# Leftover modulation weights loaded as 1 MB pairs during the routing, and the norm steps on Pool taken one block at a time

## The chip, the cores and the metric

The kernel runs on one core of a Trainium2 chip. The metric is device time in microseconds (us): the median of three runs of the kernel before is 2188.16 us, from 2187.27 to 2190.72. Durations below come from one profiled execution of its own.

## The reference, cut to what matters

Two transformer blocks run one after the other on 256 tokens of width 1024, all in fp32.

The first block is a mixer (mLSTM and Hyena) followed by an expert-choice mixture of experts: 16 experts, each of which takes its 32 best tokens. Its shifts, scales and gates are "modulations", a conditioning vector times a 1024 x 6144 matrix.

The second block has depth 2 and two streams, a latent stream `x` (the output of the first block) and a context stream of 256 tokens that does not depend on `x`. For every layer and both streams there are six modulation groups of 1024 values:

```python
mod = (silu_c @ w_ada[l] + b_ada[l])[:, None, :]
mod_c = silu_cc @ w_ada[l] + b_ada[l]
...
x = layer_norm(ALPHA * x + g1 * (o @ w_out[l]), ln1_g[l], ln1_b[l])
x = layer_norm(ALPHA * x + g2 * swiglu(modulate(x, sh2, sc2), w_ffn_in[l], w_ffn_out[l]), ln2_g[l], ln2_b[l])
```

## The kernel before, in words

The work has three stages.

**Phase A** (`phase_a`, up to 262 us of the span) is the mixer of the first block. TensorE multiplies from 1 MB weight tiles, tag `w`, a ring of 4 buffers. `gemm2` inserts background steps with `bg(2)`: each step is one `next` of the generator `later`, that is, one 128 x 1024 slice of a modulation matrix. A step loads 512 KB with `mtile` (L805, issued at L396 in `wtile`) into the ring `wm` of 4 buffers (in phase A also `wx`, 2 buffers) and multiplies it in 4 matmuls (L406). Eight steps make a group, which ends in `modout` and `modend`: an ACT copy `mrow`, two transposes, two small DVE additions. A group and its end share the single PSUM buffer "f". `later` has 12 groups, 96 steps; phase A takes 74 of them. The last 22 (six of one group, and two whole groups) are left for `ctx_path`, which runs them first (`yield from self.later`).

**The experts.** `moe_route` (L1045) computes the router's softmax, picks the 32 best tokens of each expert in a chain of small DVE operations with four PE transposes, and gathers the tokens into `xsel` with 32 matmuls. Then `moe` walks the 16 experts: 24 weight tiles of 1 MB each, 384 in all, loaded by `etile` (L1107) into 7 buffers in turn (4 of tag `w`, 3 of tag `wb`, the latter in memory that phase A gives back at its end). `run` interleaves the context stream: `ctx_path` is a generator whose steps carry costs, and after each of the first 366 expert tiles it is advanced to a share of `total`, 524.4 units; the 22 leftover steps count 0.5 each. A context step is put behind the expert tile's last matmul with `issue_after`.

**The latent stream** (`x_path`) runs after the last expert. In its feed-forward (`ffn`, L1808), 22 hidden blocks of 128 columns are computed one after the other. TensorE works in 48 fp32r matmuls on a block, after ACT (`wh`) and DVE (`wl`) have split its weights in a high and a low half. The end of a block is `fin(j, pp)`: DVE forms `lt` from PSUM, ACT writes the silu to `hj` (2 buffers), DVE multiplies into `hj`, ACT copies its high half to `hidh`, and Pool subtracts it to get the low half, `hidl`, in `evac` (L256). Only then is the `hj` buffer free. With each `fin`, `next(app)` traces one step of `apply` (L1338): three Pool operations that normalise one of 8 blocks of the residual `xT`, for use much later in the second half of the feed-forward. Nothing but the tracing order stands between these operations and the `hidl` ones.

All weight loads are issued from the one in-order queue of SP. Instructions of an engine run in the order in which the scheduler put them; `issue_after(ins)` puts what it encloses behind `ins` on the same engine, with no wait of its own.

Of the kernel before, what the change touches and what calls it, by code (L numbers as in the profile page):

```python
# [218 lines left out]
class _B:  # L219
# [104 lines left out]
    def T(self, pool, shape, tag, bufs=1, dt=F32):  # L324
        self.n += 1
        return pool.tile(shape, dt, tag=tag, name=f"{tag}_{self.n}", bufs=bufs)
# [72 lines left out]
    def modvec(self, psp, wd, lhs, bias, outs, groups, get=None):  # L399

        for g in groups:
            ps = self.P(psp)
            for k in range(8):
                w = get(g, k) if get else self.mtile(wd[128 * k:128 * k + 128, 1024 * g:1024 * g + 1024])
                for c in range(4):
                    self.mm(ps[32 * c:32 * c + 32, 0:256], lhs[:, k, :], w[:, 256 * c:256 * c + 256], k == 0, k == 7)  # L406
                yield 0.5
            self.all(self.modout(self.wm, psp, ps, bias, outs, g))
# [36 lines left out]

    def run(self):
        nc, tc, d = self.nc, self.tc, self.d
        self.wbufs = {"w": 4, "wm": 4, "wx": 2, "wb": 3, "wd": 2, "split": 4}
        with ExitStack() as es:
            E = lambda **k: es.enter_context(tc.tile_pool(**k))  # L450
            self.cp = E(name="cp", bufs=1)
            self.res = E(name="res", bufs=1)
            pm, pa = "b", "a"
            self.ws = E(name="ws", bufs=5, side="right")
            with tc.tile_pool(name="ps", bufs=1, space=PSUM) as self.pp, \
                    tc.tile_pool(name="wm", bufs=4, side="right") as self.wm:
                self.pbufs = {"b": 2, "a": 3, "g": 2, "f": 1}
                self.setup()
                with tc.tile_pool(name="A", bufs=1) as ap:
                    self.wx = ap  # L460
                    self.phase_a(ap, pm, pa)
                    self.wx = None
                if self.stop == "A":
                    return
                kp = E(name="kv", bufs=1)
                self.kvpool(kp)
                with tc.tile_pool(name="M", bufs=1) as mp, tc.tile_pool(name="WB", bufs=1) as self.wb:
                    self.moe_route(mp, pm)
                    with tc.tile_pool(name="X", bufs=1, side="right") as xp:

                        g = self.ctx_path(xp, pa)
                        done, total = 0.0, 524.4
                        for i, _ in enumerate(self.moe(mp, pm)):
                            while done < total * (i + 1) / 366:

                                with tc.issue_after(self.elm.ins):
                                    c = next(g, None)
                                if c is None:
                                    break
                                done += c  # L480
                        for c in g:
                            done += c
            if self.stop == "X":
                return
            self.pbufs = {"g": 2, "l": 2, "s": 2, "t": 1, "o": 1}
            with tc.tile_pool(name="ps2", bufs=1, space=PSUM, reuse_waits="tile") as self.pp, \
                    tc.tile_pool(name="C", bufs=1, reuse_waits="tile") as xp:
                self.x_path(xp)
# [41 lines left out]
    def phase_a(self, ap, pm, pa):  # L530
# [271 lines left out]
                    self.act(sq, self.xtok[t][g], AF.Square, accum_out=self.ssq[:, t, g:g + 1])  # L802
        self.dump("x1T", self.xT)

    def mtile(self, src):  # L805

        self.mn = getattr(self, "mn", -1) + 1
        a, b = self.wbufs["wm"], self.wbufs["wx"] if self.wx else 0
        return self.wtile(src, self.wx, "wx", 1024) if self.mn % (a + b) >= a else self.wtile(src, self.wm, "wm", 1024)
# [235 lines left out]
    def moe_route(self, mp, pm):  # L1045
        nc, T, P, col = self.nc, self.T, self.P, self.col
        m = self.mod1
        gs = self.gs2
        self.xsel = T(mp, [128, 8, 512], "xsel")
        self.Pg = T(mp, [128, 2, 16, 32], "Pg")  # L1050
        with self.tc.tile_pool(name="MR", bufs=1) as rp:
            sm = T(rp, [128, 2], "sm")
            self.tt(sm, self.ssq[:, :, 0], self.ssq[:, :, 1], ALU.add)
            r = self.rsqrt(rp, sm, 2, 1.0 / 1024, 1e-6, "rm")
            lg = T(rp, [128, 2, 16], "lg")
            for t in range(2):
                self.stt(lg[:, t], self.lgp[:, 16 * t:16 * t + 16], r[:, t:t + 1], self.cst, ALU.mult, ALU.add)

            xt = tuple(T(rp, [128, 2, 1024], "xt" + c, 1, F32R) for c in "hl")
            for t in range(2):  # L1060
                for g in range(2):
                    pt, c = self.xtok[t][g], slice(512 * g, 512 * g + 512)
                    self.act(xt[0][:, t, c], pt, scale=r[:, t:t + 1])
                    self.stt(xt[1][:, t, c], pt, r[:, t:t + 1], xt[0].bitcast(F32)[:, t, c], ALU.mult, ALU.subtract)
            mx = T(rp, [128, 2], "mx")
            nc.vector.tensor_reduce(mx, lg, AX.X, ALU.max)
            aff = T(rp, [128, 2, 16], "aff")
            self.tt(aff, lg, mx.unsqueeze(2).to_broadcast([128, 2, 16]), ALU.subtract)
            self.act(aff, aff, AF.Exp)
            nc.vector.tensor_reduce(sm, aff, AX.X, ALU.add)  # L1070
            nc.vector.reciprocal(sm, sm)
            self.tt(aff, aff, sm.unsqueeze(2).to_broadcast([128, 2, 16]), ALU.mult)
            pa = P(pm)
            for t in range(2):
                self.tp(pa[:16, 128 * t:128 * t + 128], aff[:, t])
            wk = T(rp, [16, 256], "wk")
            nc.vector.tensor_copy(wk, pa[:16, :256])
            m8 = T(rp, [16, 8], "m8")
            for r in range(4):
                nc.vector.max(m8, wk)  # L1080
                nc.vector.match_replace(wk, m8, wk, -1.0)
            msk = T(rp, [16, 256], "msk")
            self.ts(msk, wk, 0.0, None, ALU.is_lt)
            sl = T(rp, [16, 256], "sl")
            nc.vector.tensor_tensor_scan(sl, self.onerow[:16], msk, 0.0, ALU.mult, ALU.add)
            self.tt(sl, sl, msk, ALU.mult)
            self.ts(sl, sl, -1.0, None, ALU.add)
            pt = P(pm)
            for t in range(2):
                self.tp(pt[:, 16 * t:16 * t + 16], sl[:, 128 * t:128 * t + 128])  # L1090
            slT = T(rp, [128, 2, 16], "slT")
            nc.vector.tensor_copy(slT, pt[:, 0:32].rearrange("p (t e) -> p t e", t=2))
            ohr = T(rp, [128, 2, 16, 32], "oh", 1, F32R)
            oh = ohr.bitcast(F32)
            for t in range(2):
                self.tt(ohr[:, t], slT[:, t].unsqueeze(2).to_broadcast([128, 16, 32]),
                        self.iota.unsqueeze(1).to_broadcast([128, 16, 32]), ALU.is_equal)
                self.tt(self.Pg[:, t], oh[:, t], aff[:, t].unsqueeze(2).to_broadcast([128, 16, 32]), ALU.mult)
            for k in range(8):
                ps = P(pm if k % 2 else "a")  # L1100
                for t in range(2):
                    for i in range(2):
                        self.mm(ps, xt[i][:, t, 128 * k:128 * k + 128], ohr[:, t].rearrange("p e s -> p (e s)"),
                                t + i == 0, t + i == 2)
                self.act(self.xsel[:, k], ps, AF.Identity, scale=gs[:, k:k + 1], bias=m[:, 24 + k:25 + k])
# [702 lines left out]
    def ffn(self, st, l, u, ax, g, feed=None):  # L1808

        p, psp, d = st["p"], st["g"], self.d  # L1810
        if st["r3"]:
            hid = (self.T(p, [128, 22, 256], "hidh", 1, F32R), self.T(p, [128, 22, 256], "hidl", 1, F32R))
# [2 lines left out]
        extra = st.get("extra") or iter(())  # L1815

        def fin(j, pp):
            h = self.T(p, [128, 256], "hj", 2)
            t, c = self.lfin(p, pp[0], ro)
            self.act(h, t, AF.Silu, bias=c)  # L1820
            t, c = self.lfin(p, pp[1], ro)
            e = self.stt(h, t, c, h, ALU.add, ALU.mult)
            self.evac(st, hid, j, h, self.nc.gpsimd)
            with self.tc.issue_after(e.ins):
                if j % 3:
                    next(extra, None)
            next(app, None)
        for j in range(22):
            yield 7.0
            w = self.wload(st, d["w_f1"][l, j].rearrange("p k a c -> p k (a c)"))  # L1830
# [24 lines left out]
        for c in range(4):  # L1855
            pp = [self.P(psp), self.P(st["S"])]
            for j0 in (0, 8, 16):
                n = min(8, 22 - j0)
# [154 lines left out]
```

## Time and profile before

| | |
|---|---|
| median of three runs | 2188.16 us |
| profiled execution | 2185.51 us |
| its span, first to last instruction | 2183.8 us |
| PE busy | 1945.7 us (89%) |
| DVE busy | 966.9 us (44%) |
| ACT busy | 636.0 us (29%) |
| POOL busy | 289.8 us (13%) |
| moved by DMA | 666.31 MB |

Busy time is a share of the whole span, and the three stages have different limits, so it is read stage by stage. The profile was read in this order: a table of windows with the DMA's rate for each, the chain of work that ended last, the issues on SP's queue, and then the engines' timelines, waits and groups inside the feed-forward of the latent stream.

### The profile page before, as it was taken

Reading aid. Unit: us, or ns where it says so; the run is one execution under the profiler, and the core shown is the slowest. Engines: PE = TensorE matmul, PEld = TensorE weight load, DVE = VectorE, ACT = ScalarE, POOL = GpSimd, SP = SyncE. Lnnn points to the kernel's source line nnn. Section 1 sums busy time; section 2 is a strip of 40 time slices with the busy share of each in tenths; the row PEclk is TensorE's granted clock in tenths of the full one; section 3 lists DMA queues with packets and bytes.
Section 4 is the critical chain, followed back from the end, with each engine's and each line's share of the span. In section 5 each row is a group of like instructions: output and inputs, shape, how many; then the busy total and the mean of one; then the engine's idle time right before and its main releaser. Section 6 shows DMA issues by size and latency. Waiting matters only on the chain.

```text
span 2183.8 us, 33015 instructions
## 1 busy us (share of the span) xinstructions
PE 1945.7 (89%) x13588; PEld 1362.4 (62%) x13588; DVE 966.9 (44%) x1919; ACT 636.0 (29%) x1096; POOL 289.8 (13%) x334
## 2 busy tenths in 40 slices
PE   8999778997677989888988899789989998998998
PEld 4687634553223555455555445287789998778998
DVE  4566421215221211101100131088689888868964
ACT  5434221013211100000000021065545445554543
POOL 0012000001000000000000000052063116206211
PEclk9999879999999999999999999789999999999999
DMA  9887769999999999999999999952247764124652
GB/s 355 299 304 280 257 239 410 415 418 410 417 416 414 415 418 415 414 415 418 414 412 415 417 384 406 409 186 88 68 157 257 240 243 144 72 85 174 227 192 87
DMA packets 133559, 666.31 MB, mean 305 GB/s; under 512 B 14624, under 2 KB 18144, under 8 KB 86944
## 3 DMA queue, kind: packets, MB, share of 16 engines
q1 hardware_dynamic: 132272, 660.38, 77.7%
q0 software_dynamic: 1136, 3.82, 0.5%
q8 instruction: 107, 1.75, 0.3%
q14 instruction: 44, 0.36, 0.0%
HBM read 663.10 MB, written 1.05 MB: 304 GB/s over the span
## 4 chain that ended last, share of the span: by engine, by line
PE 50%; DMA 23%; DVE 8%; POOL 2%; ACT 2%; issue 2%; SPq 0%; POOLq 0%; ACTq 0%; DVEq 0%
PE ps L236 48%; DMA wm<-in_w_f 5%; DMA w<-in_w_up 4%; DMA w<-in_w_down 3%; DMA wb<-in_w_down 3%; DMA wb<-in_w_up 3%; PE ps L306 2%; DMA wm<-in_w_out 2%; DVE wl L319 1%; POOL xT L319 1%; DMA wm<-in_w_ada 1%; DVE ll L322 1%; DMA wd<-in_w_ada 1%; DMA wm<-in_w_in 1%; DMA wb<-in_w_gate 1%
## 5 line engine op out<-in xcount | busy, mean ns | idle before, releaser
L236 PE MATMUL ps<-u,wm 128*128 128x256 f32 (+1 forms) x1168 | 272.0, 392 | 5.7 <-DMA wm<-in_w_f 2.0
L236 PEld LDWEIGHTS ps<-u,wm 128*128 128x128 f32 (+1 forms) x1168 | 222.8, 194 | 76.6 <-issue 20.5
L319 DVE TENSOR_TENSOR wl<-w,wh 128x1024 fp32r<-128x1024 f32 (+1 forms) x194 | 238.6, 1238 | 55.2 <-ACT wh L309 54.8
L236 PE MATMUL ps<-lh,wh 128*128 128x258 f32 x848 | 245.2, 290 | 7.6 <-DVE lt L319 7.6
L236 PE MATMUL ps<-ll,wh 128*128 128x258 f32 x848 | 244.8, 289 | 5.2 <-DVE ll L322 5.2
L236 PE MATMUL ps<-lh,wl 128*128 128x258 f32 x848 | 244.2, 288 | 5.4 <-DVE wl L319 3.9
L309 ACT ACTIVATE wh<-w 128x1024 fp32r<-128x1024 f32 (+1 forms) x196 | 200.1, 1029 | 163.4 <-PE ps L236 153.3
L236 PE MATMUL ps<-w,xsel 128*32 128x512 f32 x1176 | 179.2, 641 | 32.2 <-DMA w<-in_w_up 26.4
L319 DVE TENSOR_TENSOR hid<-hid,ps 128x256 f32<-128x256 f32 (+1 forms) x38 | 20.2, 532 | 345.6 <-ACT hid L309 263.8
L236 PEld LDWEIGHTS ps<-lh,wh 128*128 128x128 f32 x848 | 164.5, 194 | 10.0 <-ACT wh L309 8.0
L236 PEld LDWEIGHTS ps<-ll,wh 128*128 128x128 f32 x848 | 165.1, 195 | 6.3 <-DVE ll L322 6.2
L236 PEld LDWEIGHTS ps<-lh,wl 128*128 128x128 f32 x848 | 164.7, 194 | 6.6 <-DVE wl L319 5.1
L236 PE MATMUL ps<-wb,xsel 128*32 128x512 f32 x872 | 128.4, 614 | 26.2 <-DMA wb<-in_w_up 20.5
L309 ACT ACTIVATE hid<-ps 128x256 f32<-128x256 f32 (+1 forms) x38 | 18.0, 474 | 388.2 <-PE ps L236 376.2
L1132 POOL COPY px<-Pg 128x256 f32<-128x256 f32 x16 | 6.4, 400 | 794.6 <-PE ps L306 779.9
L236 PE MATMUL ps<-w,hidT 128*32 128x512 f32 x584 | 82.6, 655 | 31.0 <-DMA w<-in_w_down 23.4
L236 PEld LDWEIGHTS ps<-w,xsel 128*32 128x32 f32 x1176 | 32.8, 111 | 115.0 <-DMA w<-in_w_up 56.5
L322 DVE SCALAR_TENSOR_TENSOR xT<-ps,mod,xT 128x256 f32<-128x256 f32 x168 | 72.8, 478 | 59.8 <-PE ps L236 59.5
L236 PE MATMUL ps<-hidh,wl 128*128 128x256 f32 x352 | 98.6, 280 | 0.6 <-DVE wl L319 0.5
L236 PE MATMUL ps<-hidh,wh 128*128 128x256 f32 x352 | 98.8, 281 | 0.0
L236 PE MATMUL ps<-hidl,wh 128*128 128x256 f32 x352 | 98.3, 279 | 0.0
L319 POOL TENSOR_TENSOR hidl<-hj,hidh 128x256 fp32r<-128x256 f32 x44 | 64.8, 1475 | 152.5 <-ACT hidh L309 152.5
(476 smaller groups left out, 3630.0 us busy)
## 6 DMA issues: line engine op xcount, KB each, us to landing
w<-in_w_gate SPq DMA_DIRECT2D x74, 1024.0 KB, 16.3
w<-in_w_up SPq DMA_DIRECT2D x73, 1024.0 KB, 15.5
w<-in_w_down SPq DMA_DIRECT2D x73, 1024.0 KB, 16.3
w<-in_w_f SPq DMA_DIRECT2D x60, 1024.0 KB, 4.9
wb<-in_w_up SPq DMA_DIRECT2D x55, 1024.0 KB, 15.3
wb<-in_w_down SPq DMA_DIRECT2D x55, 1024.0 KB, 16.6
wb<-in_w_gate SPq DMA_DIRECT2D x54, 1024.0 KB, 15.7
wm<-in_w_ada SPq DMA_DIRECT2D x76, 512.0 KB, 6.4
```

What stands on the lines that cost most here:

```text
L236: self.lm = self.nc.tensor.matmul(out, lhsT, rhs, start=start, stop=stop)
L306: self.nc.tensor.transpose(out, in_, self.ident[:k, :k])
L309: self.nc.scalar.activation(out, in_, func, **kw)
L319: return (eng or self.nc.vector).tensor_tensor(out, a, b, op)
L322: return (eng or self.nc.vector).scalar_tensor_tensor(out, in0, s, in1, op0, op1)
L1132: nc.gpsimd.tensor_copy(px.rearrange("p t (r s) -> p t r s", r=4), self.Pg[:, :, e, :].unsqueeze(2).to_broadcast([128, 2, 4, 32]))
```

## The change

Four edits. (1) `later` is run to its end in `run`, between the parts of `moe_route`, which becomes a generator with two pauses: before the softmax, and before the gather matmuls. The second part is traced after eight of the 22 leftover steps, the gather after all of them and behind their last matmul. (2) These steps load two slices at a time, 1 MB, into the experts' 7 buffers, and their loads stand behind the last 512 KB load on SP's queue. (3) `total` drops by 11 units, 22 x 0.5. (4) In `fin`, the step of `apply` is put behind the `hidl` operation of the same block, and `hj` gets a third buffer.

```diff
@@ modvec
-                w = get(g, k) if get else self.mtile(wd[128 * k:128 * k + 128, 1024 * g:1024 * g + 1024])
+                w = get(g, k) if get else self.mrows(wd, g, k)
@@ run
+        self.mwide, self.mpair = False, None
...
-                    self.moe_route(mp, pm)
+                    route = self.moe_route(mp, pm)
+                    next(route)
+
+                    self.mwide = True
+                    for n, _ in enumerate(self.later):
+                        if n == 8:
+                            next(route)
+                    with tc.issue_after(self.lm.ins):
+                        self.all(route)
...
-                        done, total = 0.0, 524.4
+                        done, total = 0.0, 513.4
@@
+    def mrows(self, wd, g, k):
+
+        c = slice(1024 * g, 1024 * g + 1024)
+        if self.mpair is not None:
+            w, self.mpair = self.mpair, None
+            return w
+        if self.mwide and k % 2 == 0:
+            with self.tc.issue_after(self.mlast.ins):
+                w = self.etile(wd[128 * k:128 * k + 256, c].rearrange("(a p) c -> p a c", p=128))
+            self.mpair = w[:, 1]
+            return w[:, 0]
+        w = self.mtile(wd[128 * k:128 * k + 128, c])
+        self.mlast = self.ld
+        return w
@@ moe_route
+            yield
             mx = T(rp, [128, 2], "mx")
...
+            yield
             for k in range(8):
                 ps = P(pm if k % 2 else "a")
@@ ffn
-            h = self.T(p, [128, 256], "hj", 2)
+            h = self.T(p, [128, 256], "hj", 3)
...
-            self.evac(st, hid, j, h, self.nc.gpsimd)
+            lo = self.evac(st, hid, j, h, self.nc.gpsimd)
             with self.tc.issue_after(e.ins):
                 if j % 3:
                     next(extra, None)
-            next(app, None)
+
+            with self.tc.issue_after(lo.ins):
+                next(app, None)
```

## Rows read from the trace of the kernel before

**Rows 1.** Windows: us, PE, PEld, DVE, ACT, POOL busy (count), clock, DMA share, GB/s

```profile
262.00:275.50 13.50, 0.58 (x2) 0.12 (x2) 9.95 (x37) 4.29 (x8) 1.50 (x2) 0.60 0.88 351
275.50:288.20 12.70, 11.08 (x44) 8.02 (x45) 3.28 (x8) 6.23 (x8) 0.88 (x2) 0.75 0.01 2
288.20:322.50 34.30, 26.02 (x242) 8.63 (x245) 5.98 (x18) 7.78 (x14) 0.48 (x2) 0.76 0.88 309
330.00:1200.00 870.00, 740.66 (x4467) 398.85 (x4467) 153.82 (x360) 92.99 (x196) 17.05 (x31) 0.95 1.02 415
```

**Rows 2.** Chain that ended last, pieces in order of time: start us, us, what

```profile
277.51 10.58 PE ps L236 x40
...
303.89 6.47 DMA wm<-in_w_ada
...
1407.19 10.55 DMA wb<-in_w_down
...
1633.56 60.12 PE ps L236 x487
```

**Rows 3.** Timeline of SP, the loads it issues: start us, us, what

```profile
208.64 0.33 SPq L396 DMA_DIRECT2D w<-in_w_gate  x1
...
232.88 0.42 SPq L396 DMA_DIRECT2D w<-in_w_gate  x1
...
240.34 2.58 SPq L396 DMA_DIRECT2D wm<-in_w_ada  x2
...
262.42 0.38 SPq L1884 DMA_DIRECT2D u<-in_ctx  x1
262.85 1.72 SPq L396 DMA_DIRECT2D wb<-in_w_gate  x3
...
290.66 28.35 SPq L396 DMA_DIRECT2D wm<-in_w_ada  x18
...
322.54 1.38 SPq L396 DMA_DIRECT2D w<-in_w_up  x3
```

**Rows 4.** Timeline of POOL, first feed-forward: first apply operations, first hidl

```profile
1608.36 4.25 POOL L319 TENSOR_TENSOR xT<-xT,ro 128x256 f32<-128x256 f32 x4 [2.54 <-ACT ro L309]
...
1628.04 0.72 POOL L319 TENSOR_TENSOR hidl<-hj,hidh 128x256 fp32r<-128x256 f32 x1
```

**Rows 5.** Waits, 1590 to 1760 us: us in total, times, longest

```profile
ACT hj L309 <- POOL hidl L319: 9.8, 1, 9.8
```

**Rows 6.** Windows, same columns, around the stalls of both feed-forwards

```profile
1628.20:1633.60 5.40, 0.60 (x3) 0.33 (x2) 4.27 (x6) 2.82 (x4) 5.30 (x6) 0.68 0.18 33
1633.60:1636.80 3.20, 3.20 (x15) 3.20 (x16) 3.10 (x6) 1.46 (x2) 0.50 (x1) 0.50 0.28 113
2003.20:2008.80 5.60, 0.81 (x4) 0.35 (x2) 4.29 (x6) 2.82 (x4) 5.50 (x7) 0.71 0.16 34
2008.80:2012.40 3.60, 3.60 (x17) 3.60 (x18) 3.50 (x7) 1.75 (x3) 0.47 (x1) 0.50 0.36 112
1640.00:1690.00 50.00, 50.00 (x420) 49.45 (x419) 48.53 (x89) 25.86 (x37) 17.12 (x9) 1.00 0.72 254
```

**Rows 7.** Windows, same columns, while phase A loads 1 MB modulation tiles

```profile
20.00:24.00 4.00, 4.00 (x6) 1.34 (x4) 1.88 (x3) 1.44 (x2) 0.00 (x0) 0.50 1.04 430
```

**Rows 8.** Groups of POOL by form, 1600 to 1640 us

```profile
L319 POOL TENSOR_TENSOR xT<-xT,ro 128x256 f32<-128x256 f32 x16 | 15.4, 994 | 2.5 <-ACT ro L309 2.5
L316 POOL TENSOR_SCALAR xT<-xT,cfg,cfb 128x256 f32<-128x256 f32 x8 | 7.3, 922 | 0.1
```

**Rows 9.** Groups of DVE by form, 1608 to 1623 us, Pool always busy

```profile
L319 DVE TENSOR_TENSOR wl<-w,wh 128x1024 fp32r<-128x1024 f32 x4 | 6.4, 1597 | 0.0
L322 DVE SCALAR_TENSOR_TENSOR lt<-ro,lc,lt 128x256 f32<-128x256 f32 x6 | 4.3, 749 | 0.0
```

**Rows 10.** Groups of DVE by form, 1660 to 1690 us, after the apply operations

```profile
L319 DVE TENSOR_TENSOR wl<-w,wh 128x1024 fp32r<-128x1024 f32 x11 | 13.4, 1218 | 0.9 <-ACT wh L309 0.9
L322 DVE SCALAR_TENSOR_TENSOR lt<-ro,lc,lt 128x256 f32<-128x256 f32 x12 | 5.8, 485 | 0.4
```

## The prediction

> **What bounds the kernel now.** Read first the windows with the DMA's rate [rows 1]. From 330 us on, through the experts, the DMA engines are busy all the time (share 1.02) and move 415 GB/s, so this stage lasts as long as its bytes take. The chain says the same at its end: the last piece before the latent stream is a load of an expert's tile, at 1407 us [rows 2]. A microsecond in which the DMA stands still before that is a microsecond of the kernel, and the windows show two such stretches. From 275.5 to 288.2 us it moves 2 GB/s: the 7 expert buffers are full, and TensorE has no `xsel` yet. Then, from 288.2 to 322.5 us, it moves only 309 GB/s, while SP issues 18 of the 22 leftover slices, one behind the other, over 28.35 us [rows 1, 3]. The chain of this stretch runs through these loads, of 6.47 us for instance [rows 2]: 4 buffers of 512 KB are too few to keep the queue full. SP's queue is in order, so the expert tiles behind the slices go on at 322.54 us only [rows 3].
>
> In the latent stream the chain is TensorE (60.12 us at a stretch from 1633.56 us, [rows 2]). Just ahead of that stretch it stalls. Pool starts the `apply` operations at 1608.36 us and gets to the first `hidl` at 1628.04 us [rows 4]; ACT waits 9.8 us for an `hj` buffer [rows 5]; from 1628.2 us TensorE is busy for 0.60 of 5.40 us, and then runs at a granted clock of 0.50, the 1.2 GHz level, for 3.2 us. The second layer repeats it at 2003.2 us [rows 6].
>
> **The loads, part by part.** From 262.0 to 322.5 us the DMA moves 13.5 x 351 + 12.7 x 2 + 34.3 x 309 = 15.4 MB [rows 1]. At 415 GB/s these 60.5 us hold 25.1 MB. The gap, 9.7 MB or 23.5 us, is the most that the first part can give. Against it stands one thing that is moved: the pairs use the expert buffers, and their loads are put behind the last 512 KB load, issued at about 242 us [rows 3]. Before, two expert tiles had gone out by then, at 208.64 and 232.88 us, beside phase A [rows 3]. That is 2.1 MB, or 5.05 us, to be loaded later. I take 23.5 - 5.05 = **18.4 us**.
>
> This asks that the DMA doesn't stop between 262 us and the first expert. By 262 us four pairs can be in the four `w` buffers, which phase A has done with by then. Then come the context input and seven pairs, 8.39 MB, 20.2 us: the last pair lands near 282.6 us. Expert tiles fill the 7 buffers in another 17.7 us, until 300.3 us. The gather matmuls, now behind the last pair, took 10.58 us [rows 2]; with 2 us for the last pair's own steps `xsel` is ready near 295 us, later than before (288.1 us) but ahead of 300.3 us. So the delay costs nothing; if that cover were gone, each microsecond past 300.3 us would cost one.
>
> Do 4 KB rows of a wide matrix run at the full rate? While phase A loads such 1 MB tiles, the window shows 430 GB/s [rows 7], so 415 stands. TensorE and DVE have room for the 22 steps: in the 13.5 us from 262 us on, TensorE is busy for 0.58 us; DVE for 9.95 us, to which three group ends of two small additions come [rows 1]. In the experts' stage the same work disappears, which is worth nothing, since the DMA sets its length. The `total` of 513.4 keeps the context stream's end at the 366th tile: nothing.
>
> **Pool's steps.** TensorE lost 5.40 - 0.60 = 4.8 us, and half of the 3.2 us at the lower clock, 1.6 us; in the second layer 5.60 - 0.81 = 4.8 us and half of 3.6 us, 1.8 us [rows 6]. Together 13.0 us, the most that the second part can give. With the new order, `hidl` of a block runs as soon as `hidh` is there, and one step of `apply`, 2 x 0.994 + 0.922 = 2.91 us [rows 8], follows; a block lasts 48 / 420 x 50 = 5.71 us [rows 6], so Pool keeps up, and with three `hj` buffers ACT has a block more to run ahead. `xT` is first used after the 22 blocks: its later end costs nothing.
>
> What is late next is DVE. After the stall it is busy for 48.53 of 50 us [rows 6], a slack of 0.17 us in a block. Beside a busy Pool its `wl` takes 1.597 instead of 1.218 us and `lt` 0.749 instead of 0.485 [rows 9, 10]; with two `wl`, two `lt`, and `hj`, which has the form of `lt`, a block loses 0.76 + 0.79 = 1.55 us when Pool never rests. The eight steps make Pool busy for 2.91 of 5.71 us: 0.79 us a block, 6.3 us a layer. Of this the kernel before had paid 14.4 / 5.71 x 1.55 = 3.9 us from 1608.3 to 1622.7 us, ahead of the stall and hidden by it. The rest, 2.4 us, less the slack of 8 x 0.17 = 1.3 us, is 1.1 us a layer. I take 13.0 - 2.2 = **10.8 us**; the bounds are 13.0, and 13.0 - 12.6 = 0.4 us if all of the contention shows.
>
> Here a rule speaks against the change. The rows show DVE operations with two SBUF inputs made longer by a third to a half beside Pool, not blocked [rows 9, 10]. The Trainium skill (page "SBUF — State Buffer", section "SBUF: two separate sides") says of the port pair that both share: "The shared pair is an exclusive lock, not a bandwidth split", and the loser waits for the whole instruction. By that rule each step of `apply` would take its full 2.91 us from DVE; the third rival works this out as a mechanism.
>
> **The sum.** 18.4 + 10.8 = 29.2 us off the profiled execution of 2185.51 us (span 2183.8 and 1.7 around it) is 2156.3 us. The median of the runs is 2.65 us above that execution: **2159 us**.
>
> **Rivals.** *The gather comes late.* TensorE takes its instructions in order, the groups share one PSUM buffer with their ends, and the ends' ACT and DVE operations stand in line with the routing's. If the 22 steps went at the pace of before, 28.35 / 18 = 1.58 us each [rows 3], they would end at 262.4 + 34.7 = 297.1 us, `xsel` at 307.6 us, and the DMA would stand still for 7.3 us. Then 11.1 + 10.8 = 21.9 us: 2166 us. For it: half of the clock while TensorE waits (0.60 in the window, [rows 1]); against it: 1 MB tiles and 7 buffers instead of 4 of 512 KB.
>
> *Pool's part gives nothing*, because DVE, at 97% [rows 6], is late instead and TensorE stalls in small pieces: 18.4 us alone, 2170 us. For it the thin slack; against it that the largest stall was a queue of 20 us on Pool, not DVE's work.
>
> *Slower: the port locks.* If each `apply` operation holds DVE for all its time, a layer loses 8 x (2.91 - 0.17) = 21.9 us and wins 6.5, so both lose 30.8 us and the loads return 18.4: 12.4 us slower, 2201 us. It decides from a share of 0.73 of Pool's time lost by DVE, where both parts cancel. The rows say 1.55 / 5.71 = 0.27 in a stretch where Pool was always busy [rows 9, 10], over 2.5 blocks.
>
> *It doesn't do what it says*: the scheduler leaves the pairs behind the routing and the loads between the same waits; then nothing moves, 2188 us, and Pool's order alone would give at most 2175.
>
> **How the numbers follow.** Forecast 0.55, late gather 0.18, no gain from Pool 0.14, the lock 0.06, not done 0.07. About 0.2% (4.4 us) is what a measurement of this kernel can tell from no change. The first three cases are faster by more, as is a third of the last, since the order on Pool alone would show: 0.89; same 0.05; slower 0.06. The range runs from both upper bounds, 23.5 + 13.0 = 36.5 us, to both lower ones, 11.1 + 0.4 = 11.5 us: 2152 to 2177 us.
>
> **What would show it.** Right: no window near 2 GB/s between 275 and 288 us and none near 309 after it; 18 loads of 512 KB after 290 us gone, the first `w_up` load some 18 us earlier; the last expert load some 18 us earlier; on Pool `hidl` and groups of three `apply` operations in turn; no wait of ACT for `hidl`; TensorE without the gap near block 5 and its clock at 1.00. Wrong: a DMA gap between 283 and 308 us (late gather), DVE at 100% with many short gaps on TensorE through the first ten blocks (no gain, or the lock), or a longer experts' stage at the same bytes, which nothing here foresees.

## The result and the profile after

The median of four runs of the changed kernel is 2150.65 us (2148.67 to 2154.66), beside 2187.72 us for the kernel before in the same session. The ratio is 0.983, with a 95% interval from 0.9813 to 0.9854. That is 37 us off; the prediction said 29 and put the low end of its range at 2152 us, 1.35 us too high. Run again later as **r_change_again**, the change took 2149.91 us, ratio 0.9836 [0.982, 0.9852].

> The change itself, once more, as the measure for the kernels beside it. Its first four runs gave 37.1 us off the kernel before; three kernels that differ from it by one thing each gave 33 to 35. If those differences are noise of the kernel before, this run gives 34 to 37 us off and lies within 2 us of them; if the order with two hj buffers, the missing norm steps or the free loads really cost 2 to 3 us, it is that much faster than they were, near 0.983.

So the gain is 37 us, a little more than in most of the runs below that leave the change nearly whole. The rest of this section compares the two profiled executions, 2185.51 us before and 2151.79 us after.

First the windows of the changed kernel (columns as in [rows 1]), over the stretches of [rows 1] and the first feed-forward, which answers to [rows 6].

```profile
262.00:275.50 13.50, 6.54 (x66) 2.25 (x62) 6.78 (x27) 4.31 (x7) 1.50 (x2) 0.72 0.97 358
275.50:288.20 12.70, 9.98 (x80) 4.21 (x76) 6.25 (x17) 0.38 (x1) 0.39 (x1) 0.50 1.03 412
288.20:322.50 34.30, 34.30 (x212) 20.70 (x205) 11.19 (x31) 16.45 (x25) 1.65 (x4) 1.00 0.97 382
300.00:312.00 12.00, 12.00 (x73) 7.59 (x73) 5.00 (x16) 4.52 (x9) 0.39 (x1) 1.00 0.89 347
330.00:1200.00 870.00, 746.52 (x4465) 399.69 (x4463) 150.82 (x353) 87.92 (x189) 15.86 (x29) 0.94 1.02 415
1606.00:1640.00 34.00, 34.00 (x285) 34.00 (x284) 33.58 (x56) 16.98 (x24) 29.17 (x23) 1.00 0.61 217
1640.00:1670.00 30.00, 30.00 (x253) 29.45 (x253) 28.21 (x55) 15.04 (x22) 8.20 (x6) 1.00 0.70 256
```

From 275.5 to 288.2 us the DMA now moves 412 GB/s where it moved 2, and 382 follow where 309 stood. The expert stage behind it has the same 415 GB/s as before. In the feed-forward TensorE (first busy column) has no gap and no stretch at the clock of 0.50.

The chain that ended last (start us, us, what; columns as in [rows 2]), in the kernel before and then in the changed one. `nc` is Pool's last operation ahead of a feed-forward, the piece of 462 or 750 matmuls is the feed-forward's second half:

```profile
1604.20 1.63 POOL nc L319
...
1693.90 55.24 PE ps L236 x462
...
1979.37 1.63 POOL nc L319
...
2069.19 89.33 PE ps L236 x750
```

```profile
1385.89 11.99 DMA w<-in_w_down
...
1584.10 1.62 POOL nc L319
1585.77 80.83 PE ps L236 x672
1666.82 55.24 PE ps L236 x462
...
1952.41 1.62 POOL nc L319
1954.08 80.81 PE ps L236 x672
2035.12 89.32 PE ps L236 x750
```

The last expert load lands at 1397.88 us; before it was 1407.19 + 10.55 = 1417.74 us [rows 2]. **The loads therefore gave 19.9 us.** The first half of each feed-forward is now one unbroken piece of TensorE. Its second half starts at 1666.82 us instead of 1693.90 us. That is 27.1 us earlier, so 7.0 more were won since `nc` (1584.10 instead of 1604.20 us). The second layer adds 7.1: from `nc` to the second half it takes 82.7 instead of 89.8 us. **Pool's order gave 14.1 us.** The two sums make 34.0, and the span is 33.8 us shorter.

SP's timeline in the changed kernel shows where the 11 pairs stand (start us, us, what):

```profile
241.79 9.37 SPq L396 DMA_DIRECT2D w<-in_w_ada  x4
251.25 0.91 SPq L396 DMA_DIRECT2D wm<-in_w_in  x2
261.39 0.38 SPq L396 DMA_DIRECT2D w<-in_w_ada  x1
262.21 1.66 SPq L396 DMA_DIRECT2D wb<-in_w_ada  x3
263.97 3.09 SPq L396 DMA_DIRECT2D w<-in_w_ada  x3
274.06 0.34 SPq L396 DMA_DIRECT2D wb<-in_w_gate  x1
274.45 0.43 SPq L1912 DMA_DIRECT2D u<-in_ctx  x1
...
301.07 8.68 SPq L396 DMA_DIRECT2D wb<-in_w_up  x2
```

The 18 issues of 512 KB that filled 28.35 us [rows 3] are gone, and `w_up` starts at 301.07 us instead of 322.54. The `wm` buffers that the slices no longer use are not idle: two tiles of the context's `w_in` go out at 251.25 us. The context's load (`u`) now comes behind all the pairs.

Pool in the first feed-forward, two blocks of the changed kernel (start us, us, what), and then its groups by form from 1590 to 1640 us:

```profile
1609.21 1.20 POOL L319 TENSOR_TENSOR hidl<-hj,hidh 128x256 fp32r<-128x256 f32 x1 [0.86 <-ACT hidh L309]
1610.38 1.88 POOL L319 TENSOR_TENSOR xT<-xT,ro 128x256 f32<-128x256 f32 x2
1612.36 1.64 POOL L316 TENSOR_SCALAR xT<-xT,cfg,cfb 128x256 f32<-128x256 f32 x1
1614.28 1.40 POOL L319 TENSOR_TENSOR hidl<-hj,hidh 128x256 fp32r<-128x256 f32 x1 [0.27 <-ACT hidh L309]
```

```profile
L319 POOL TENSOR_TENSOR xT<-xT,ro 128x256 f32<-128x256 f32 x16 | 18.8, 1178 | 0.6
L316 POOL TENSOR_SCALAR xT<-xT,cfg,cfb 128x256 f32<-128x256 f32 x8 | 12.7, 1592 | 0.8
```

Where 20 us of `apply` stood ahead of the first `hidl` [rows 4], `hidl` and one step of three operations now take turns. The wait of ACT for `hidl` [rows 5] is no longer in the list. A step takes 2 x 1.178 + 1.592 = 3.95 us instead of the 2.91 us of [rows 8], and with a `hidl` of 1.16 us it still fits into a block of 5.71 us.

### The profile page after: what moved, and what is told of

It is laid out like the page before. It is cut to its first block, busy times and chain, and to the rows that moved or that the text cites. A ratio compares the mean times of both kernels' runs of the same rounds, so it can differ in the third digit from the quotient of the medians.

```text
span 2150.0 us, 32998 instructions
## 1 busy us (share of the span) xinstructions
PE 1943.2 (90%) x13588; PEld 1363.0 (63%) x13588; DVE 970.0 (45%) x1919; ACT 634.2 (29%) x1095; POOL 302.1 (14%) x334
## 3 DMA queue, kind: packets, MB, share of 16 engines
HBM read 663.10 MB, written 1.05 MB: 309 GB/s over the span
## 4 chain that ended last, share of the span: by engine, by line
PE 61%; DMA 25%; DVE 7%; ACT 3%; issue 3%; POOL 1%; SPq 0%; POOLq 0%; ACTq 0%; DVEq 0%
PE ps L236 59%; DMA w<-in_w_up 7%; DMA w<-in_w_down 4%; DMA wm<-in_w_f 3%; DMA wb<-in_w_down 3%; PE ps L306 2%; DMA wb<-in_w_up 2%; DMA wm<-in_w_in 2%; DVE wl L319 1%; DMA wm<-in_w_out 1%; DMA wd<-in_w_ada 1%; DMA w<-in_w_gate 1%; POOL AT L319 1%; DVE PT L319 1%; ACT E L309 0%
## 5 line engine op out<-in xcount | busy, mean ns | idle before, releaser
L319 DVE TENSOR_TENSOR wl<-w,wh 128x1024 fp32r<-128x1024 f32 (+1 forms) x194 | 244.8, 1270 | 49.6 <-ACT wh L309 49.4
L236 PE MATMUL ps<-hid,wm 128*128 128x256 f32 x352 | 85.0, 402 | 0.9 <-DMA wm<-in_w_f 0.9
```

Of the source, the lines that this page charges most:

```text
L236: self.lm = self.nc.tensor.matmul(out, lhsT, rhs, start=start, stop=stop)
L319: return (eng or self.nc.vector).tensor_tensor(out, a, b, op)
```

## The experiments

Every run is compared with runs of the kernel before on the same chip, whose medians lie from 2186.22 to 2187.91 us. "Off" means off that median.

### The two parts alone

**e1_routing_only** takes the two edits of `ffn` out of the change:

```diff
-            h = self.T(p, [128, 256], "hj", 3)
+            h = self.T(p, [128, 256], "hj", 2)
...
-            with self.tc.issue_after(lo.ins):
-                next(app, None)
+            next(app, None)
```

> The load part alone, with the feed-forward's Pool order and its two hj buffers as before. Theory: the whole first-part gain is the DMA's standing time that is filled, so this is 20 us faster than the kernel before (the shift of the last expert load in the two profiles, 1417.8 to 1397.9 us), and both stalls of TensorE in the feed-forwards are back. Rival: the step of the prediction stands, 18.4 us, and what was more than forecast came from the Pool part.

Measured: 2166.26 us, ratio 0.9905 [0.9888, 0.9923], 21.6 us off. The last expert load lands at 1397.2 us, as with the whole change, and TensorE's stall is back in both feed-forwards.

**e2_pool_only** is the kernel before with these two edits alone:

```diff
-            h = self.T(p, [128, 256], "hj", 2)
+            h = self.T(p, [128, 256], "hj", 3)
...
-            self.evac(st, hid, j, h, self.nc.gpsimd)
+            lo = self.evac(st, hid, j, h, self.nc.gpsimd)
...
-            next(app, None)
+            with self.tc.issue_after(lo.ins):
+                next(app, None)
```

> The Pool part alone on the kernel before. Theory: each feed-forward gets its 7.0 us back whole, 14 us faster, and DVE's contention with Pool costs TensorE nothing. Rival: the prediction's 10.8 us, with contention of 1.1 us a layer.

Measured: 2174.01 us, ratio 0.9939 [0.9924, 0.9954], 13.9 us off. The two gains add up to 35.5 us, about the whole, so the parts don't depend on each other. By these medians each was priced too low by about 3 us, but the interval of e1 still holds the 18.4 us of the prediction.

### Which of Pool's two edits

**e3_order_two_hj** keeps the new order and goes back to two `hj` buffers:

```diff
-            h = self.T(p, [128, 256], "hj", 3)
+            h = self.T(p, [128, 256], "hj", 2)
```

> The whole change but for the third hj buffer. Theory: the order alone does it, since hidl now follows hidh at once and frees its buffer 1 to 2 us later: the time of the whole change, 34 to 37 us faster than before. Rival: beside a busy Pool hidl comes late enough to make ACT wait for hj again, and 2 to 7 us are lost.

Measured: 2152.63 us, ratio 0.9846 [0.9827, 0.9865], 35.3 us off. In its trace ACT no longer waits for `hidl`, and TensorE is busy without a gap from 1587 to 1666 us and from 1955 to 2034 us, in the two first halves.

**e4_three_hj_only** keeps the buffer and goes back to the old order:

```diff
-            with self.tc.issue_after(lo.ins):
-                next(app, None)
+            next(app, None)
```

> The whole change but for the order of Pool: the third hj buffer stays. Theory: Pool still does its norm steps in one go of 20 us, and a third buffer lets DVE go on for one more block of 5.7 us, so that of 7.0 us of stall a layer 1 to 2 remain: 31 to 34 us faster than before. Rival: the order is what counts, the buffer gives nothing, and this is 20 us faster than before, as the load part alone.

Measured: 2157.41 us, ratio 0.9864 [0.9844, 0.9884], 30.5 us off. The order does the work: it needs no third buffer. The buffer alone gets some 9 of the 14 us, because Pool reaches `hidl` no earlier in its queue, but ACT has a block more in hand. Pool's timeline of e4 and the wait from 1575 to 1735 us:

```profile
1585.61 4.25 POOL L319 TENSOR_TENSOR xT<-xT,ro 128x256 f32<-128x256 f32 x4 [2.52 <-ACT ro L309]
...
1608.85 0.73 POOL L319 TENSOR_TENSOR hidl<-hj,hidh 128x256 fp32r<-128x256 f32 x1
```

```profile
ACT hj L309 <- POOL hidl L319: 6.5, 1, 6.5
```

Pool still runs through `apply` operations for 23 us ahead of its first `hidl`, and ACT's wait falls from the 9.8 us of [rows 5] to 6.5. By the trace 3.2 us of the stall are left in each layer, more than the 1 to 2 us expected.

### What Pool costs DVE

**e7_no_apply** leaves the norm steps out of both feed-forwards, so Pool has only `hidl` to do:

```diff
-                            app = self.apply(p, ax, ro, st["cf"])
+                            app = iter(())
```

> The whole change, with the norm steps on Pool left out of both feed-forwards (the residual is not normalised there, which is the part of the computation that is missing), so that Pool does only hidl. Theory: the contention of Pool and DVE is real (wl 1.51 us on average beside Pool) but fits into DVE's slack, and TensorE loses nothing by it: the time of the whole change within 1 us. Rival: the 2.2 us for contention that the prediction charged are still in the time, or up to 4 us: that much faster.

Measured: 2153.32 us, ratio 0.985 [0.9831, 0.987], 33.3 us off. Without the steps the kernel is no faster than with them. DVE by form from 1593 to 1640 us, first in the change, then in e7, and e7's window:

```profile
L319 DVE TENSOR_TENSOR wl<-w,wh 128x1024 fp32r<-128x1024 f32 x16 | 24.2, 1514 | 0.0
L322 DVE SCALAR_TENSOR_TENSOR lt<-ro,lc,lt 128x256 f32<-128x256 f32 x15 | 8.7, 581 | 0.3
```

```profile
L319 DVE TENSOR_TENSOR wl<-w,wh 128x1024 fp32r<-128x1024 f32 x17 | 21.0, 1236 | 1.5 <-ACT wh L309 1.5
L322 DVE SCALAR_TENSOR_TENSOR lt<-ro,lc,lt 128x256 f32<-128x256 f32 x18 | 9.0, 507 | 0.4
```

```profile
1606.00:1640.00 34.00, 34.00 (x285) 34.00 (x285) 31.89 (x58) 16.79 (x24) 8.81 (x6) 1.00 0.71 249
```

The contention is real and has the size that was foretold. `wl` takes 0.278 us more in the change and `lt` 0.074, and the operation on `hj` of the same form took 622 against 480 ns. Per block that is 2 x 0.278 + 2 x 0.074 + 0.142 = 0.85 us of DVE, against the 0.79 worked out from [rows 9, 10]. But TensorE has 285 matmuls in this window in both kernels, and no gap in either; its piece of 672 matmuls takes 80.83 us in the change and 80.82 us in e7. In e7 DVE is busy for 31.89 of 34 us, a slack of 0.35 us in a block of 5.71. The change works at 33.58 of 34 and falls a little behind: 16 `wl` and 15 `lt` of this form instead of 17 and 18 from 1593 to 1640 us. It makes this up afterwards, at 28.21 of 30 us. TensorE runs off what DVE had prepared ahead.

### The loads

**e5_half_mb** keeps the new order of work but loads the slices in 512 KB again:

```diff
-                    self.mwide = True
+                    self.mwide = False
```

> The whole change, but the 22 leftover slices are loaded one by one, 512 KB each, into the 4 wm buffers instead of as pairs into the expert buffers; they still run beside the routing. Theory: the place alone is not enough. Four buffers keep the DMA at some 309 GB/s as before; 18 slices, three expert tiles and the context input, 13.6 MB, end near 300 us, the gather near 310, and the DMA stands still in between because the expert buffers are full: 8 to 12 us of the load part are lost, some 24 us faster than before instead of 36. Rival: the place is all, and the time is that of the whole change.

Measured: 2162.08 us, ratio 0.9888 [0.9868, 0.9908], 24.5 us off. Its windows:

```profile
275.50:288.20 12.70, 8.04 (x67) 2.52 (x62) 8.56 (x24) 0.38 (x1) 0.39 (x1) 0.63 0.88 308
288.20:300.00 11.80, 9.32 (x62) 3.02 (x55) 0.14 (x2) 0.38 (x1) 0.00 (x0) 0.50 0.95 351
...
312.00:322.50 10.50, 10.50 (x63) 7.35 (x63) 3.20 (x11) 2.59 (x6) 0.00 (x0) 1.00 0.45 147
```

This is the late gather of the first rival, made on purpose. With four buffers of 512 KB the DMA moves 308 to 351 GB/s and the gather ends near 307 us. From 312 us on it moves 147 GB/s: the expert buffers are full, and from 311.79 us TensorE does 32 matmuls of the context, 7.17 us in which it gives no buffer free.

**e6_pairs_in_place** does the other half: pairs of 1 MB, but behind the whole of the routing, where the slices were before.

```diff
-                    route = self.moe_route(mp, pm)
-                    next(route)
+                    self.all(self.moe_route(mp, pm))
...
-                    for n, _ in enumerate(self.later):
...
-                        done, total = 0.0, 513.4
+                        done, total = 0.0, 524.4
```

> The whole change, but the leftover slices stay where they were, behind the routing in the context stream; only their size and their buffers change (1 MB pairs, 7 buffers). Theory: the 12.7 us in which the DMA stands still stay, and 9.4 MB go at 415 instead of 309 GB/s, which is worth 8 us; with the Pool part's 14 us this is some 22 us faster than before. Rival: the size is all, 36 us faster.

Measured: 2170.55 us, ratio 0.9925 [0.9906, 0.9944], 16 us off, of which Pool's order makes 14. The larger loads alone gave 2 us, where 8 were expected. One of its windows:

```profile
275.50:288.20 12.70, 9.94 (x32) 7.96 (x33) 4.19 (x9) 4.76 (x7) 0.39 (x1) 0.65 0.10 40
```

The DMA stands still from 275.5 us as before, since nothing is multiplied beside the routing. The pairs also sit in expert buffers: four of the seven hold pairs when the routing ends, so less expert weight is on the chip. Neither half does it alone: the pairs need the routing's time, and the routing's time needs loads that keep the queue full.

**e8_loads_free** takes away the rule that the pairs' loads stand behind the last 512 KB load, so that some can go out beside phase A, as the two expert tiles of [rows 3] did:

```diff
-            with self.tc.issue_after(self.mlast.ins):
-                w = self.etile(wd[128 * k:128 * k + 256, c].rearrange("(a p) c -> p a c", p=128))
+            w = self.etile(wd[128 * k:128 * k + 256, c].rearrange("(a p) c -> p a c", p=128))
```

> The whole change, with the pairs' loads no longer put behind the last 512 KB load: the first go out near 208 us, as the first expert tiles did before. Theory: the bytes missing at 262 us beside the kernel before (1.0 MB by the two profiles, not the 2.1 MB of the prediction) come back: 2 to 3 us faster than the whole change. Rival: nothing, because the experts' buffers are then full earlier and the DMA waits longer for the gather (371 GB/s from 300 to 322 us already).

Measured: 2152.98 us, ratio 0.9845 [0.9825, 0.9865], 33.6 us off: nothing gained. In this execution phase A ends later, with the router's last matmul (`ps<-wrs,xT`) at 263.77 us instead of 260.49, so times are counted from there. The matmuls of the first pair for a `wb` buffer now stand ahead of both transposes of `aff`, TensorE waits 5.5 us for that pair instead of 2.86, and the transposes start 11.5 us behind the router instead of 7.9. The last expert load lands 1136.5 us behind it, and 1137.4 us in the change: what was loaded early gives at most 1 us here.

### What still held the DMA after 300 us

In the change the DMA moves only 347 GB/s from 300 to 312 us. Three edits tried to fill this. **e9_gather_free** lets the gather start before the last modulation:

```diff
-                    with tc.issue_after(self.lm.ins):
-                        self.all(route)
+                    self.all(route)
```

> The gather matmuls are no longer put behind the last modulation's matmuls. In the change xsel is ready at 297 us, 3 us later than the routing chain alone would give, and from 300 to 322.5 us the DMA moves 371 instead of 415 GB/s, which is 22.5 x 44 / 415 = 2.4 us of loading. Theory (the cover of the gather was used up): the gather starts near 282 us, the window from 300 to 322.5 us shows over 390 GB/s, and 1.5 to 2.5 us are won on the change. Rival (the pairs' buffers are now freed later, since the last group's matmuls stand between the gather's): nothing is won, the low rate only moves to another window.

Measured: 2157.62 us, ratio 0.9863 [0.9849, 0.9878], 29.1 us off, some 8 us slower than the change. In the traces 3.0 us of this are a later last expert load (1400.85 us), and 3.6 lie in the latent stream, which the edit does not touch (last section). **e10_route_at_5** traces the routing's second part earlier:

```diff
-                        if n == 8:
+                        if n == 5:
```

> The second part of the routing is traced after six of the 22 leftover steps instead of nine, so the transposes of aff stand ahead of a modulation that waits 2.86 us for its load in the change. Theory: aff, sl and with them the last groups come 2 to 3 us earlier, xsel near 294.5 us, and 1.5 to 2.5 us are won on the change. Rival: the last group waits for its own loads (the last pair lands near 283 us), then xsel stays near 297 us and nothing is won.

Measured: 2150.47 us, ratio 0.9839 [0.9823, 0.9856], 36.3 us off, no faster than r_change_again beside it. **e11_free_at_5** is e8 and e10 together.

> Two things together: the routing's second part after six steps, and the pairs' loads no longer put behind the last 512 KB load. The free loads alone won nothing (33.6 us off the kernel before): their 2.5 us of earlier expert bytes were lost while xsel was late. Theory: with the routing earlier both show, 3 to 5 us better than the change. Rival: the DMA's rate after 300 us, not xsel, is the limit; then it is within 1 us of the change.

Measured: 2154.81 us, ratio 0.9855 [0.9839, 0.9871], 32 us off, so the 3 to 5 us did not come; its wait for the first `wb` pair is 5.4 us long, as in e8. The window of e9, then that of e4, a kernel that equals the change up to the latent stream:

```profile
300.00:312.00 12.00, 12.00 (x73) 7.48 (x72) 3.40 (x11) 2.80 (x6) 0.00 (x0) 1.00 0.71 273
```

```profile
300.00:312.00 12.00, 12.00 (x66) 6.72 (x65) 2.45 (x8) 0.87 (x2) 0.00 (x0) 1.00 0.97 379
```

Executions differ here. The change, r_change_again, e1, e3, e4 and e7 are the same up to the latent stream, yet in these six traces the first expert matmul comes between 293.30 us (e4) and 297.01 us (the change), and this window moves 347 to 394 GB/s. In e9 it comes at 294.8 us, and the window is far worse. TensorE's timeline of the change says why, and SP's waits from 298 to 312 us with it:

```profile
297.01 1.06 PE L236 MATMUL ps<-wb,xsel 128*32 128x512 f32 x8
298.01 2.00 PE L306 MATMUL ps<-pc,u 128*128 128x128 f32 x16
299.94 1.06 PE L236 MATMUL ps<-wb,xsel 128*32 128x512 f32 x8
...
301.21 7.14 PE L236 MATMUL ps<-u,wm 128*128 128x256 f32 x32
308.29 1.07 PE L236 MATMUL ps<-wb,xsel 128*32 128x512 f32 x8
```

```profile
SPq L396 <- PE ps L236: 8.9, 3, 7.9
```

Behind the second expert tile stand 32 matmuls of the context, 7.14 us. For that long no expert buffer comes free, and SP waits 7.9 us in one piece. In e9 only one expert tile stands ahead of them, and the wait is 11.3 us.

Three more runs asked whether these matmuls or `xsel` are the limit. **e12_ctx_later** starts the context stream after eight expert tiles, its load with it:

```diff
-                            while done < total * (i + 1) / 366:
+                            while done < total * (i - 7) / 358:
```

> The context stream starts after the eighth expert tile instead of the first; its load of 1 MB goes later with it. Theory (the first context matmuls, 7.14 us on TensorE between the second and the third expert tile, keep buffers from coming free): SP's wait of 7.9 us near 301 us is gone, the window from 300 to 322.5 us shows over 400 GB/s instead of 371, 2.4 us won there; but the 1 MB that was loaded while the seven buffers were full now comes on top, 2.5 us, so about the time of the change, 2150 us. Rival (xsel is the limit): the window stays near 371 GB/s and it is some 2.5 us slower than the change.

**e13_ctx_hold** leaves the load and its transposes in place and holds the matmuls alone:

```diff
-                            while done < total * (i + 1) / 366:
+                            while done < (0.01 if i < 8 else total * (i - 7) / 358):
...
+        yield 0.01
         yield from self.later
```

> As before, but the context's load and its first transposes stay where the change has them; only its matmuls wait until after the eighth expert tile. Theory (these matmuls are the limit): the window from 300 to 322.5 us shows over 400 GB/s with xsel near 297 us as in the change, the last expert load lands about 2.4 us earlier, and the time is 2 to 2.5 us below the change's. Rival (xsel): nothing moves.

**e14_hold_at_5** is e13 with the earlier routing.

> The held context matmuls and the routing's second part after six steps, together. The earlier routing alone had filled the window from 300 to 322.5 us (417 and 422 GB/s) and brought the last expert load some 2 us forward without a gain in the median. Theory (both cure the same 2 us): the last load lands as with one of them, and the time is within 1 us of the better of them, 2148 to 2150 us. Rival (two separate limits): 2 us more, near 2146 us.

Measured: e12 2155.32 us, 0.985 [0.9833, 0.9868]; e13 2152.74 us, 0.9839 [0.982, 0.9858]; e14 2151.81 us, 0.9836 [0.9815, 0.9857]. The window of e12, then of e13:

```profile
300.00:312.00 12.00, 7.44 (x52) 1.68 (x53) 1.21 (x3) 0.60 (x1) 0.40 (x1) 0.85 1.02 416
```

```profile
300.00:312.00 12.00, 8.25 (x47) 2.75 (x44) 1.22 (x6) 4.07 (x5) 0.00 (x0) 0.86 1.01 419
```

Two pairs of traces tell the two apart. The first expert matmul is at 297.20 us in e12 and at 297.01 in the change, and the window moves 416 GB/s against 347. It is at 293.34 us in e13 and at 293.30 in e4, and the window moves 419 against 379. With `xsel` at the same time, the window is full only where the context's matmuls are held: in these traces they are the limit, not `xsel`. e10 is not explained by this: its 32 matmuls stand where they did, from 297.03 us, and its window is full all the same (417 GB/s), while e4, with these matmuls from 297.51 us, has 379.

e12's median is also 5 us above the 2150 us of its theory. In its trace phase A ends 1.9 us later than in the change, and the last load lands 0.8 us later from there; the rest is open.

None of the gains shows in the medians: the window is worth at most (415 - 347) x 12 / 415 = 2 us, and 0.9 from the 384 GB/s of r_change_again, where 4.4 us is what can be told from nothing. A single trace does not show it either. e13's last expert load lands at 1395.83 us, 2 us ahead of the change's, but in the six equal kernels this load lands between 1395.90 us (e4) and 1398.19 us (e7), since the end of phase A moves as well. Counted from the router's last matmul it lands after 1136.5 to 1138.1 us in the six, after 1136.9 in e13, 1135.6 in e10, 1134.6 in e14 and 1141.5 in e9. The earlier routing may thus be worth 1 to 3 us of loading, shown by one execution each; the held matmuls alone are worth nothing that can be seen. No run beat the change beyond the uncertainty.

## Why the prediction missed, point by point

The mechanisms were those foretold, and none of the rivals came true. The time came out 8.35 us below the forecast, outside the range, because the errors of its terms, each taken as a whole, all lay on the same side. On the profiled executions the gain is 33.7 us instead of 29.2. The first point below needs TensorE's timeline of the kernel before, at the stall of the first feed-forward:

```profile
1627.94 0.28 PE L236 MATMUL ps<-ll,wh 128*128 128x258 f32 x1
1632.02 0.55 PE L236 MATMUL ps<-lh,wh 128*128 128x258 f32 x1 [3.81 <-DVE lt L319]
1633.56 0.58 PE L236 MATMUL ps<-lh,wl 128*128 128x258 f32 x1 [0.99 <-DVE wl L319]
...
1636.95 0.28 PE L236 MATMUL ps<-lh,wl 128*128 128x258 f32 x1
```

- **Pool's part, 10.8 foretold, 14.1 measured** in the traces and 13.9 alone (e2). This is the step that failed most, twice over. First, the upper bound of 13.0 was not one. It took a window from 1628.2 us on and counted the 0.60 us in which TensorE is busy there as useful. In the lines above, ahead of 1627.94 us and from 1636.95 us on, a matmul starts each 0.12 us. In the 9.0 us between, 17 start, which is 2.0 us of work: 7.0 us are lost, not 6.4, and the feed-forward shrank by 7.0 and 7.1 us. Second, the 2.2 us taken off for DVE's contention were not lost at all (80.83 us for the first half with the steps, 80.82 without, e7). The price of the contention was right, its effect on the end was not. The slack of 0.17 us a block was read from 1640 to 1690 us [rows 6], where DVE was catching up after the stall: it made 19 `wl` there, and TensorE used 17.5. Undisturbed the slack is 0.35 us (e7), and work prepared ahead covers the rest.
- **The loads, 18.4 foretold, 19.9 measured.** Two sizes were off, in opposite ways. The early expert tiles were priced at 5.05 us; from 200 to 262 us the DMA moved 221 instead of 238 GB/s, so only 1.05 MB or 2.5 us were missing, since context tiles took the freed `wm` buffers. The standing time was not all won: the gap of 23.5 us gave 18.8, plus 1.7 from 322.5 to 330 us. Together 20.5 - 2.5 = 18.0. The other 2 us are 0.8 GB/s over the 1060 us behind 330 us, less than the rounded rates can show, and stay open. Counted from the router's last matmul, which came 0.85 us earlier in this execution than in the one before, the last load is 19.0 us earlier, and 18.3 to 20.3 us over the six traces named above: this term is off by little more than its scatter.
- **`xsel` near 295 us and its cover.** It came between 293.3 and 297.0 us in the six traces of equal kernels, but by two errors that cancel. In the change the gather starts at 289.27 us instead of 284.6; TensorE had waited 2.86 us for a load on the way. And it takes 7.7 us, not 10.58: that piece of 40 matmuls [rows 2] holds the first 8 of the experts beside the 32 of the gather. That the delay costs nothing held up to 300 us. What came after it was not foreseen: the context's first 32 matmuls, the limit of the window that follows.
- **From the profiled execution to the median, +2.65.** Before, the profiled execution lay below its median, and afterwards it lay 1.14 us above it. This offset is scatter of one execution and should not have been carried over; it makes 3.8 of the 8.35 us.
- **The range.** Its low end was the sum of the two upper bounds plus that same offset. Without the offset it would have been 2149 us.
- **The port lock.** Opposed to the rows, and it did not happen. By the Trainium skill (page "SBUF — State Buffer", section "SBUF: two separate sides"), of a DVE operation with two SBUF inputs and a Pool operation that reads SBUF, the one that starts first gets the shared port pair for its whole instruction, and the other is blocked. The trace does not show that here: beside a Pool at 29.17 of 34 us, `wl` takes 1.514 us and not 1.236 plus the rest of a Pool operation of 1.178 or 1.592 us, and the kernel loses nothing. DVE lost 0.85 us to a step; for the rival to make the kernel slower it needed 0.73 x 2.91 = 2.1 us.

## What to carry to other kernels

Where a stage lasts as long as its bytes, look for stretches in which the DMA stands still and put work there whose loads are large enough to keep the queue full; one without the other gave 2 or 10 us here, both gave 20. An engine that is off the critical path can stop the one on it by the order of its queue alone: interleave long side work with the short operations that others wait for, before adding buffers. When the slack of an engine is read from a profile, read it in a stretch that is not catching up after a stall, and treat the distance of one execution from the median as scatter.

## What the runs showed of the hardware that was not expected

Pool pays for the shared time too. Its `apply` operations took 1.178 and 1.592 us beside DVE's new rhythm, against 0.994 and 0.922 us [rows 8].

The latter half of the kernel is not equally long from one execution to the next, though its instructions are the same. From the second half of the first feed-forward to the start of the second one (1666.82 to 1954.08 us in the change) eleven traces take 286.8 to 288.1 us, but e9 takes 290.9 and e14 291.0. e14 joins the edits of e10 and e13, which take 287.3 and 286.8. In e9 TensorE's matmuls stand in the same order as in the change: one stretch of weight loads ends 1.8 us later, and behind it TensorE's granted clock differs. The stretch behind the feed-forward, in the change and then in e9:

```profile
1757.40:1811.80 54.40, 46.98 (x370) 45.07 (x370) 46.29 (x86) 32.56 (x48) 32.54 (x33) 0.97 0.42 146
```

```profile
1761.80:1816.40 54.60, 48.64 (x369) 46.64 (x369) 46.44 (x86) 32.76 (x48) 32.69 (x33) 0.94 0.41 146
```

The mean granted clock is 0.94 instead of 0.97, TensorE is busy for 1.7 us longer with the same work, and the 143 us that follow take 1.6 us longer at 0.98 instead of 0.99. TensorE stands still for 7.4 and 6.0 us of this stretch, and the clock behind it differs although the instructions do not; why it does was not tried. So a gain of 2 us in the loads, as was hoped for in e10 and e13, is smaller than what one execution differs from another.
